# Four pairs of eight by seven products in both feed-forwards of a Conformer block, with other summed tiles

## The chip, the cores and the metric

The kernel runs on one core of one Trainium2 chip. The metric is the device time of one execution in microseconds, from the first to the last instruction with what lies around it. A core has a matrix engine (PE, whose loads of the stationary operand are listed apart as PEld), a vector engine (DVE), an activation engine (ACT), GpSimd (POOL), a sync engine (SP) that issues most loads here, and 16 DMA engines. Each engine works through its own instructions in the order in which they were written into its queue, and waits at an instruction until the semaphores it names have arrived.

## The reference

One layer on 256 tokens of 2048 features: a feed-forward, two mixers side by side (a convolution module and a spatial gating unit), cross-attention into 256 memory tokens, a second feed-forward, and a final norm. All arithmetic is float32. The part that matters here:

```python
def swiglu_ffn(h, w_in, w_out):
    gate, up = jnp.split(h @ w_in, 2, axis=-1)
    return (jax.nn.silu(gate) * up) @ w_out

h = rms_norm(x, ffn1_norm[l])
x = x + MACARON_SCALE * swiglu_ffn(h, ffn1_w_in[l], ffn1_w_out[l])
...
h = rms_norm(x, ffn2_norm[l])
x = x + MACARON_SCALE * swiglu_ffn(h, ffn2_w_in[l], ffn2_w_out[l])
```

`w_in` is 2048 x 11264 and `w_out` 5632 x 2048, so the two feed-forwards hold most of the layer's weights.

## The kernel before

**Three matmuls for one product.** Every float32 operand is split into a rounded half and what is left. ACT casts the rounded half, DVE subtracts it from the original to get the rest, and a product is three matmuls: rounded by rounded, rounded by rest, rest by rounded (`three`, L317 to L319; `by_two`, L330 to L333). For a weight tile this is `parts` (L396 the cast, L397 the subtraction); the tile of 128 x 1024 goes into one of a few buffers, `hl`, `ring` and, in the first feed-forward, `more`, that are used in turn: six in the first feed-forward, five in the second. Loads go to `raw` buffers (four, and parts of the tile `spare`), also in turn, issued by SP (L407).

**Groups.** The product `h @ w_in` is done in 11 groups, j = 0 to 10. A group takes 512 columns of gate and 512 of up, and adds over 16 tiles of 128 features (k = 0 to 15), that is, 8 pairs. Group 0 is done tile by tile, 12 matmuls a tile. Groups 1 to 10 follow a pattern over their pairs, `SCSCSCCC` before the change:

- **C** (`eight`): a pair of two tiles by the plain eight products, 24 matmuls. Each tile is split by `parts`, unless it is a *summed* tile.
- **S** (`seven`): the 2 x 2 block product (two token halves by two column halves) by seven products instead of eight, 21 matmuls. DVE forms sums of the weight blocks first: L464 and L465 into `sums`, L471 into the first tile's buffer, L478 into the second's; and `parts` splits `sums`, the first tile, the second tile and half of it again. The sums on the token side are made once (`sides`) during group 0.

**Summed tiles** (`summed`) spare DVE the subtraction: ACT writes the negative of the rounded half into the place of the rest (L425) and the rounded half beside it (L426), and a DMA issued by GpSimd (L427) adds the weights from memory onto the negative. These tiles have buffers of their own, `hl_s` and a second one. In the second feed-forward the second buffer is given up from group 8 on, where its space is taken by the results of groups 9 and 10. `sums_at` lists which tiles are made this way, three in a group, k = 2, 7, 13.

**The end of a group.** Seven banks of PSUM collect the products, named 1 to 7, and 8. After the last S pair, `joins_sevens` reads banks 1, 6, 5, 7 and 5 again (ACT copies bank 1 at L515; DVE adds at L516 to L519). After the last pair DVE adds banks 2, 4, 3 and 8 (L544, four times) and `give` applies the gate (ACT L504, DVE L506, two of each). The next group takes the banks in the order in which they come free.

**The output product** of the first feed-forward (`out_block`, twice) uses the same two kinds of pairs over 22 pairs; its loads turn among four `raw`, four `raws_out`, and, from step 8 of the first block on, two `raw_out` buffers, whose space is that of the last groups' results and comes free when these have been transposed. The tile `sums_out` lies there too.

The order on every engine is made by the scheduler of the framework, from the order of the code; `tc.issue_after` ties an instruction behind another.

Of the kernel before, what the change touches and what calls it, by code (L numbers as in the profile page):

```python
# [11 lines left out]
F32 = mybir.dt.float32  # L12
# [5 lines left out]
P = 128  # L18
# [15 lines left out]
SCALE = float(HD) ** -0.5  # L34


PATTERNS = ("SCSCSCCC", "SCSCSCCC")

SUMMED = ((2, 7, 13), (2, 7, 13))

# [35 lines left out]
def layer(ctx: ExitStack, tc: tile.TileContext, a: dict):  # L78
# [262 lines left out]
    class FeedForward:  # L341
# [60 lines left out]
        def raw(self, j, k):  # L402
            i = self.raw_at % (4 + len(self.raws))
            self.raw_at += 1
            raw = wraw.tile([P, 1024], F32, name="raw") if i < 4 else self.raws[i - 4]

            nc.sync.dma_start(out=raw, in_=self.w_in[j, :, k] if j < NG else self.w_out[j - NG, :, k])  # L407
            return raw

        def buffer(self, at):  # L410
# [7 lines left out]
        def summed(self, at):  # L418

            if at >= len(self.sums_at):  # L420
                return
            j, k = self.sums_at[at]
            raw, hl = self.raws_summed[self.buffer(at)], self.hls[self.buffer(at)]
            nc.sync.dma_start(out=raw, in_=self.w_in[j, :, k])
            nc.scalar.activation(out=hl[:, 1], in_=raw, func=AF.Copy, scale=-1.0)  # L425
            nc.scalar.copy(out=hl[:, 0], in_=raw)  # L426
            nc.gpsimd.dma_start(out=hl[:, 1], in_=self.w_in[j, :, k], accum_op=ALU.add)  # L427

        def sides(self, i):

# [90 lines left out]
        def group(self, j, r, after=()):  # L521
            if self.pair and j == NG - 2:
                both = self.high_pool.tile([P, 2, 2, G], F32, name="h_pair", tag="pair")
                self.h[NG - 2:] = [both[:, i] for i in range(2)]
            b = {}
            self.begun = set()
            self.banks(b, "57612348")
            after = list(after)
            p1, u2, u4, u5 = self.u
            n = len(self.pattern)  # L530
            for p, c in enumerate(self.pattern):
                if c == "S":
                    self.seven(j, p, b, p == self.spairs[-1])
                    if p == self.spairs[-1]:
                        self.joins_sevens(b, p1, u2, u4, u5)
                else:
                    late = p > self.spairs[-1] and len(after) > 0
                    self.eight(j, p, b, p == n - 1, late)
                    if p > self.spairs[-1] + 1:
                        for _ in range(2):  # L540
                            if after:
                                after.pop(0)()
            for acc, u in (("2", p1), ("4", u2), ("3", u4), ("8", u5)):
                nc.vector.tensor_tensor(out=u, in0=u, in1=b[acc], op=ALU.add)  # L544
            self.give(j, (p1, u2), (u4, u5), r)
# [58 lines left out]
        def run(self, before, after, root, more=None, early=False):  # L604
            acc = token_accs()
            sums = self.pattern_sums
            self.sums_at = [(j, k) for j in range(1, NG) for k in sums if j < NG - 1 or k < min(14, sums[-1])]
            for k in range(KD):
                if k == 0 and early:
                    w = self.early(before)  # L610
                else:
                    before(k)
                    w = self.parts(self.raw(0, k))
                begin = [(t, g) for t in range(2) for g in range(2)] if k == 0 else []
                by_two(acc, self.x_hl[:, k], w[:, 0], w[:, 1], k, begin, k == KD - 1)
                after(k)
                if k == 13:
                    r = root()
                    nc.scalar.activation(out=st.tile([P, 1], F32, name="warm"), in_=ones[:, 0:1], func=AF.Silu)
                    self.summed(0)  # L620
            self.give(0, [acc[t][0] for t in range(2)], [acc[t][1] for t in range(2)], r)
            if more is not None:
                more()
            if len(self.hls) > 1:
                self.summed(1)
            turns = [self.turn(i) for i in range(2 * NG)]
            for j in range(1, NG):
                if j < NG - 1:
# [52 lines left out]
    with ExitStack() as stack:  # L681
# [7 lines left out]
        def x_more(k):  # L689
            if k == 6:  # L690
                nc.sync.dma_start(out=pv, in_=a["pv"])
            if k in (2, 4, 6, 8):
                x_squares(k // 2 - 1)
            if k in (6, 9, 12):
                ff.sides(k // 3 - 2)

        def x_root():
            nc.vector.tensor_tensor(out=r_x, in0=tot[:, 0], in1=tot[:, 1], op=ALU.add)
# [48 lines left out]
        def turns_first(i):  # L747
# [8 lines left out]
            if i == 8:  # L756
                stack.enter_context(ff.late)
                ff.high.close()
                pool = rest["pool"] = stack.enter_context(tc.tile_pool(name="ffn1", bufs=1, reuse_waits="tile"))
                ff.sums = pool.tile([P, 1024], F32, name="sums_out")  # L760
                ff.raws += [pool.tile([P, 1024], F32, name=f"raw_out{q}") for q in range(2)]

        def result():
            return rest["pool"].tile([P, 2, 2 * G], F32, name="o", bufs=2)
# [2 lines left out]
            return [turning(o, 2 * i * P, joins(8 * n + 2 * i)) for i in range(4)]  # L767

        o = ff.out_block(0, result, turns_first, next_turn)
        ff.raws = ff.raws[4:]  # L770
        xT = xt.tile([P, KD, T], F32, name="xT", tag="x")
        for k in range(0, KD, 8):
            nc.gpsimd.dma_start(out=xT[:, k:k + 8], in_=a["xT"][:, k:k + 8])
# [412 lines left out]
    with ExitStack() as stack:  # L1186
# [13 lines left out]

        h = ff.of
        def first_beside(k):
            if k in (6, 9, 12):
                ff.sides(k // 3 - 2)

        turns = ff.run(lambda k: None, first_beside, lambda: rms_cols(ss, D, "r_x2"))
        put(0.3, *[turn(0, i, j) for i in range(4) for j in range(8)])
# [153 lines left out]
```

## Time and profile before

| what | us |
|---|---|
| median of 3 runs | 2098.36 |
| lowest and highest of them | 2094.91, 2098.84 |
| the profiled execution | 2097.01 |
| its span, from the first to the last instruction | 2095.2 |

The granted clock of the matrix engine is 0.999 of full speed over the span. In a row of a timeline the first number is the start in us from the span's start, the second the duration, then the engine, the source line and the operation with its output and inputs. In rows of waits the three numbers are the sum in us, the count and the longest. In rows of windows each engine's busy time is followed by the count of its instructions.

The first feed-forward's groups 1 to 9 lie at about 51 to 424 us, its output product at about 466 to 730 us, the second feed-forward's groups 1 to 9 at about 1425 to 1799 us.

### The profile page before, as it was taken

What the parts mean: (1) busy time and instruction counts of PE and PEld (TensorE: products, weight loads), DVE (VectorE), ACT (ScalarE), POOL (GpSimd) and SP (SyncE); (2) the same over time, 40 slices, a digit from 0 to 9 for tenths busy, and PEclk for the clock granted to TensorE, in tenths of its full rate; (3) what the DMA queues carried; (4) which work ended last, traced back from release to release, by engine and by line L of the source; (5) the groups of instructions that cost most, each with busy time, mean ns of one, the idle gap of its engine ahead of it and who ended that gap; (6) DMA issues with size and microseconds to landing.
All of it is one profiled execution on the core that took longest, in us unless ns stands there. A gap on an engine that the chain in (4) does not pass through costs nothing.

```text
span 2095.2 us, 26732 instructions
## 1 busy us (share of the span) xinstructions
PE 2080.0 (99%) x9765; PEld 1738.5 (83%) x9765; DVE 1621.0 (77%) x2300; ACT 1175.0 (56%) x1472; POOL 67.7 (3%) x83
## 2 busy tenths in 40 slices
PE   9999999999999999999999999999999999999998
PEld 8888888888788888888888898888888888888886
DVE  7888887877777679989877666778888878787754
ACT  8665666555546554445664455556665656554443
POOL 0000000000000000000000000000000000000000
PEclk9999999999999999999999999999999999999999
DMA  9787778755457566555555544677777777556664
GB/s 366 242 260 249 227 226 263 229 182 202 169 201 233 181 237 203 183 180 185 181 195 191 186 157 130 215 269 221 233 242 245 225 221 235 176 163 203 195 193 152
DMA packets 122532, 442.35 MB, mean 211 GB/s; under 512 B 13600, under 2 KB 13984, under 8 KB 122016
## 3 DMA queue, kind: packets, MB, share of 16 engines
q1 hardware_dynamic: 113184, 407.08, 56.4%
q0 software_dynamic: 8640, 32.51, 8.3%
q8 instruction: 76, 1.25, 0.2%
q10 hardware_dynamic: 576, 1.06, 0.1%
q14 instruction: 56, 0.46, 0.1%
HBM read 438.49 MB, written 2.10 MB: 210 GB/s over the span
## 4 chain that ended last, share of the span: by engine, by line
PE 81%; issue 15%; DMA 2%; POOL 1%; ACT 1%; DVE 1%; SPq 0%; DVEq 0%; POOLq 0%; ACTq 0%
PE acc L331 9%; PE acc L333 9%; PE acc L330 9%; PE acc L204 8%; PE acc L203 8%; PE acc L202 8%; PE acc L153 8%; PE acc L161 4%; PE acc L318 2%; PE acc L319 2%; PE acc L317 2%; PE aux L305 1%; POOL hl_s L427 1%; PE acc L1278 1%; PE acc L1277 1%
## 5 line engine op out<-in xcount | busy, mean ns | idle before, releaser
L123 ACT CAST hl<-raw 128x1024 fp32r<-128x1024 f32 (+1 forms) x315 | 327.1, 1040 | 356.1 <-PE acc L204 194.7
L124 DVE TENSOR_TENSOR hl<-raw,hl 128x1024 fp32r<-128x1024 f32 (+1 forms) x315 | 381.2, 1212 | 166.8 <-ACT hl L123 165.4
L397 DVE TENSOR_TENSOR hl<-raw,hl 128x1024 fp32r<-128x1024 f32 (+1 forms) x144 | 164.6, 1145 | 51.2 <-ACT hl L396 49.9
L396 ACT CAST hl<-raw 128x1024 fp32r<-128x1024 f32 (+1 forms) x144 | 141.0, 988 | 110.2 <-PE acc L333 51.4
L397 DVE TENSOR_TENSOR hl<-spare,hl 128x1024 fp32r<-128x1024 f32 (+1 forms) x128 | 146.9, 1152 | 37.3 <-ACT hl L396 34.6
L396 ACT CAST hl<-spare 128x1024 fp32r<-128x1024 f32 (+1 forms) x128 | 126.2, 993 | 73.3 <-PE acc L333 25.4
L331 PE MATMUL acc<-hl,x_hl 128*128 128x512 f32 x408 | 148.2, 391 | 0.1
L330 PE MATMUL acc<-hl,x_hl 128*128 128x512 f32 x408 | 142.4, 391 | 0.0
L333 PE MATMUL acc<-hl,x_hl 128*128 128x512 f32 x408 | 126.6, 389 | 0.0
L396 ACT CAST ring<-spare 128x1024 fp32r<-128x1024 f32 (+1 forms) x81 | 80.5, 998 | 59.3 <-issue 20.4
L397 DVE TENSOR_TENSOR ring<-spare,ring 128x1024 fp32r<-128x1024 f32 (+1 forms) x81 | 93.3, 1157 | 14.8 <-ACT ring L396 13.6
L203 PE MATMUL acc<-hl,x_hl 128*128 128x512 f32 x256 | 100.6, 393 | 0.0
L203 PE MATMUL acc<-hl,m_hl 128*128 128x512 f32 x256 | 100.3, 392 | 0.0
L204 PE MATMUL acc<-hl,m_hl 128*128 128x512 f32 x256 | 100.2, 392 | 0.0
L204 PE MATMUL acc<-hl,x_hl 128*128 128x512 f32 x256 | 99.9, 390 | 0.0
L331 PE MATMUL acc<-ring,x_hl 128*128 128x512 f32 x248 | 91.4, 389 | 0.0
L202 PE MATMUL acc<-hl,m_hl 128*128 128x512 f32 x256 | 90.9, 392 | 0.0
L202 PE MATMUL acc<-hl,x_hl 128*128 128x512 f32 x256 | 90.2, 392 | 0.0
L330 PEld LDWEIGHTS acc<-hl,x_hl 128*128 128x128 f32 x408 | 76.6, 188 | 16.2 <-ACT hl L396 0.4
L333 PEld LDWEIGHTS acc<-hl,x_hl 128*128 128x128 f32 x408 | 76.7, 188 | 16.0
L331 PEld LDWEIGHTS acc<-hl,x_hl 128*128 128x128 f32 x408 | 76.3, 188 | 16.4 <-DVE hl L397 0.8
L330 PE MATMUL acc<-ring,x_hl 128*128 128x512 f32 x248 | 88.8, 389 | 0.0
(515 smaller groups left out, 5115.2 us busy)
## 6 DMA issues: line engine op xcount, KB each, us to landing
spare<-in_ffn_w_in SPq DMA_DIRECT2D x185, 512.0 KB, 6.8
raw<-in_ffn_w_in SPq DMA_DIRECT2D x156, 512.0 KB, 6.3
raw<-in_ffn_w_out SPq DMA_DIRECT2D x135, 512.0 KB, 4.0
hl_s<-in_ffn_w_in POOLq DMA_DIRECT2D x44, 512.0 KB, 8.7
raw<-in_w_mix_vg SPq DMA_DIRECT2D x32, 512.0 KB, 4.5
raw<-in_w_k SPq DMA_DIRECT2D x32, 512.0 KB, 3.6
raw<-in_w_v SPq DMA_DIRECT2D x32, 512.0 KB, 4.3
raw<-in_w_mix_out SPq DMA_DIRECT2D x32, 512.0 KB, 4.6
```

What stands on the lines that cost most here:

```text
L123: nc.scalar.copy(out=hl[:, 0, :size], in_=raw[:, :size])
L124: newest[0] = nc.vector.tensor_tensor(out=hl[:, 1, :size], in0=raw[:, :size], in1=hl[:, 0, :size].bitcast(F32), op=ALU.subtract)
L153: done = nc.tensor.matmul(acc, lhsT=hi[:, k], rhs=xs[k], start=first and k == 0, stop=last and k == kk - 1, skip_group_check=True,)
L161: done = nc.tensor.matmul(acc[:, 0], lhsT=lo[:, k], rhs=xs[k][:, 0], start=False, stop=last and k == kk - 1, skip_group_check=True,)
L202: nc.tensor.matmul(acc[t], lhsT=x[:, 0, s], rhs=hi[:, k], start=k0 + k == 0, stop=False)
L203: nc.tensor.matmul(acc[t], lhsT=x[:, 0, s], rhs=lo[:, k], start=False, stop=False)
L204: nc.tensor.matmul(acc[t], lhsT=x[:, 1, s], rhs=hi[:, k], start=False, stop=k0 + k == nk - 1)
L330: nc.tensor.matmul(acc[t][g], lhsT=x[:, 0, s], rhs=hi[:, cols[g]], start=(t, g) in first, stop=False)
L331: nc.tensor.matmul(acc[t][g], lhsT=x[:, 0, s], rhs=lo[:, cols[g]], start=False, stop=False)
L333: nc.tensor.matmul(acc[t][g], lhsT=x[:, 1, s], rhs=hi[:, cols[g]], start=False, stop=last)
L396: self.cast = nc.scalar.copy(out=hl[:, 0, :n], in_=raw[:, :n])
L397: newest[0] = nc.vector.tensor_tensor(out=hl[:, 1, :n], in0=raw[:, :n], in1=hl[:, 0, :n].bitcast(F32), op=ALU.subtract)
```

## The change

The pattern of groups 1 to 9 becomes `SCSCSCSC` in both feed-forwards: the seventh pair goes from C to S. Group 10 keeps `SCSCSCCC` (`LAST`). The summed tiles are k = 2, 6, 10, 14 in the first feed-forward (2, 6, 10 in its group 10). In the second they are 2, 7, 11 in groups 1 to 7, and 2, 10 in groups 8 to 10. The token-side sums are made for four pairs, after tiles 4, 7, 10 and 13 of group 0. The first two summed tiles are tied behind the last load and the last cast that stand ahead of them in the code (`summed_then`). The two `raw_out` buffers join the turn after the first output block instead of at its step 8, and replace the four `raws_out` there.

```diff
-PATTERNS = ("SCSCSCCC", "SCSCSCCC")
-
-SUMMED = ((2, 7, 13), (2, 7, 13))
+PATTERNS = ("SCSCSCSC", "SCSCSCSC")
+
+LAST = "SCSCSCCC"
+
+SUMMED = ((2, 6, 10, 14), (2, 7, 11))
+ALONE = (2, 10)
+
+SIDES = (4, 7, 10, 13)
...
-            nc.sync.dma_start(out=raw, in_=self.w_in[j, :, k] if j < NG else self.w_out[j - NG, :, k])
+            self.load = nc.sync.dma_start(out=raw, in_=self.w_in[j, :, k] if j < NG else self.w_out[j - NG, :, k])
...
+        def summed_then(self, at):
+
+            with tc.issue_after(self.load.ins), tc.issue_after(self.cast.ins):
+                self.summed(at)
...
-            n = len(self.pattern)
-            for p, c in enumerate(self.pattern):
+            pattern = self.pattern if j < NG - 1 else LAST
+            n, done = len(pattern), pattern.rindex("S")
+            for p, c in enumerate(pattern):
                 if c == "S":
-                    self.seven(j, p, b, p == self.spairs[-1])
-                    if p == self.spairs[-1]:
+                    self.seven(j, p, b, p == done)
+                    if p == done:
                         self.joins_sevens(b, p1, u2, u4, u5)
...
+            if self.pair:
+
+                self.sums_at = [at for at in self.sums_at if at[0] < 8] + [(j, k) for j in range(8, NG) for k in ALONE]
...
-                    self.summed(0)
+                    self.summed_then(0)
...
-                self.summed(1)
+                self.summed_then(1)
...
-            if k in (6, 9, 12):
-                ff.sides(k // 3 - 2)
+            if k in SIDES:
+                ff.sides(SIDES.index(k))
...
-                ff.raws += [pool.tile([P, 1024], F32, name=f"raw_out{q}") for q in range(2)]
+                rest["raws"] = [pool.tile([P, 1024], F32, name=f"raw_out{q}") for q in range(2)]
...
-        ff.raws = ff.raws[4:]
+        ff.raws = rest["raws"]
```

DVE at the end of group 1 of the second feed-forward, before the change (a row is a source line, an operation, and its output and inputs; `acc` and `aux` are banks of PSUM, `hl` and `ring` weight buffers, `h_...` the group's result):

```order
L518 TENSOR_TENSOR spare<-spare,aux 128x512
L397 TENSOR_TENSOR hl<-spare,hl 128x1024
L519 TENSOR_TENSOR spare<-spare,acc 128x512
L464 TENSOR_TENSOR spare<-raw 128x512
L465 TENSOR_TENSOR spare<-raw 128x512
L397 TENSOR_TENSOR hl<-spare,hl 128x1024
L471 TENSOR_TENSOR raw<-spare,raw 128x512
L397 TENSOR_TENSOR hl<-spare,hl 128x1024
L478 TENSOR_TENSOR spare<-spare 128x512
L397 TENSOR_TENSOR ring<-spare,ring 128x512
L544 TENSOR_TENSOR spare<-spare,acc 128x512 x4
L506 SCALAR_TENSOR_TENSOR h_11165<-spare,r_x_11436,h_11165 128x512
```

The same place in the changed kernel, whose lines stand some ten further down (L526 to L529 are the joins, L555 the last adds, L402 the split, L474, L475, L481 and L488 the sums, L516 the gate):

```order
L528 TENSOR_TENSOR spare<-spare,aux 128x512
L402 TENSOR_TENSOR ring<-spare,ring 128x1024
L481 TENSOR_TENSOR raw<-spare,raw 128x512
L555 TENSOR_TENSOR spare<-spare,acc 128x512 x2
L529 TENSOR_TENSOR spare<-spare,acc 128x512
L488 TENSOR_TENSOR spare<-spare 128x512
L516 SCALAR_TENSOR_TENSOR h_11233<-spare,r_x_11512,h_11233 128x512
L555 TENSOR_TENSOR spare<-spare,acc 128x512 x2
L402 TENSOR_TENSOR ring<-raw,ring 128x1024
L402 TENSOR_TENSOR hl<-spare,hl 128x512
L402 TENSOR_TENSOR hl<-spare,hl 128x1024 x2
```

The last join, which stood eight rows ahead of the last adds with a whole pair's sums and splits between, now stands between the second and the third of them, and of the next group's first pair of seven the last sum and its split come behind.

SP in the output blocks of the first feed-forward, before the change:

```order
L407 DMA raw<-in_ffn_w_out 128x1024 x3
L407 DMA raws_out<-in_ffn_w_out 128x1024 x4
L407 DMA raw<-in_ffn_w_out 128x1024 x4
L407 DMA raws_out<-in_ffn_w_out 128x1024 x4
L407 DMA raw_out_3961<-in_ffn_w_out 128x1024
L407 DMA raw_out_3962<-in_ffn_w_out 128x1024
L407 DMA raw_out_3961<-in_ffn_w_out 128x1024
L407 DMA raw<-in_ffn_w_out 128x1024 x2
```

And in the changed kernel:

```order
L412 DMA raws_out<-in_ffn_w_out 128x1024 x4
L412 DMA raw<-in_ffn_w_out 128x1024 x4
L412 DMA raws_out<-in_ffn_w_out 128x1024 x4
L412 DMA raw<-in_ffn_w_out 128x1024 x4
L412 DMA raws_out<-in_ffn_w_out 128x1024 x3
L412 DMA raw_out_4024<-in_ffn_w_out 128x1024
L412 DMA raw_out_4025<-in_ffn_w_out 128x1024
L412 DMA raws_out<-in_ffn_w_out 128x1024 x2
```

The first load into a `raw_out` buffer stood behind 29 loads of the output product's weights and stands behind 30; before, it was for a tile of the first block, now for one of the second.

More of the change, by code (lines that the diff above doesn't have):

```diff
@@ L529, in group @@
             p1, u2, u4, u5 = self.u
-            n = len(self.pattern)
-            for p, c in enumerate(self.pattern):
+            pattern = self.pattern if j < NG - 1 else LAST
+            n, done = len(pattern), pattern.rindex("S")
+            for p, c in enumerate(pattern):
                 if c == "S":
-                    self.seven(j, p, b, p == self.spairs[-1])
-                    if p == self.spairs[-1]:
+                    self.seven(j, p, b, p == done)
+                    if p == done:
                         self.joins_sevens(b, p1, u2, u4, u5)
                 else:
-                    late = p > self.spairs[-1] and len(after) > 0
+                    late = p > done and len(after) > 0
                     self.eight(j, p, b, p == n - 1, late)
-                    if p > self.spairs[-1] + 1:
+                    if p > done + 1:
                         for _ in range(2):
@@ L1202, in first_beside @@
         def first_beside(k):
-            if k in (6, 9, 12):
-                ff.sides(k // 3 - 2)
+            if k in SIDES:
+                ff.sides(SIDES.index(k))
         turns = ff.run(lambda k: None, first_beside, lambda: rms_cols(ss, D, "r_x2"))
```

## The prediction

> **What bounds the kernel now.** I read the page first, for the engine that is never idle, then the busy time by stretches over the groups that the change touches, then single starts on TensorE and VectorE there, and last who waits for whom.
>
> ```profile
> span 2095.2 us, 26732 instructions
> PE 2080.0 (99%) x9765; PEld 1738.5 (83%) x9765; DVE 1621.0 (77%) x2300; ACT 1175.0 (56%) x1472; POOL 67.7 (3%) x83
> PE 81%; issue 15%; DMA 2%; POOL 1%; ACT 1%; DVE 1%; SPq 0%; DVEq 0%; POOLq 0%; ACTq 0%
> ```
>
> PE is busy for 2080.0 of 2095.2 us, and the chain that ends last runs along it. A busy PE may hide slow matmuls, so the groups come next: nine of the first feed-forward, nine of the second.
>
> ```profile
> core 0: us, PE busy (x) PEld busy (x) DVE busy (x) ACT busy (x) POOL busy (x), PEclk, DMA share, GB/s
> 51.00:424.50 373.50, 373.50 (x1649) 309.27 (x1649) 309.63 (x371) 232.89 (x257) 24.38 (x28) 1.00 0.77 240
> 1425.00:1799.00 374.00, 372.18 (x1640) 307.26 (x1638) 307.92 (x368) 231.72 (x250) 22.66 (x26) 1.00 0.76 236
> ```
>
> PE has no gap in the first and 1.8 us in the second, at full clock. VectorE is the runner-up: 309.63 / 9 = 34.4 us of a group of 41.5, 307.92 / 9 = 34.2 in the second, so it idles 7.1 and 7.3 us a group. ACT (25.8 us a group) and the DMA share (0.77) have more room. The same product of three groups in a row gives PE's price of a matmul:
>
> ```profile
> 133.55 0.39 PE L317 MATMUL acc<-hl,ring 128*128 128x512 f32 x1
> ...
> 175.03 0.39 PE L317 MATMUL acc<-hl,ring 128*128 128x512 f32 x1
> ...
> 216.51 0.39 PE L317 MATMUL acc<-hl,ring 128*128 128x512 f32 x1
> ```
>
> A group is 3 pairs of 21 matmuls and 5 of 24, 183 in all; two groups take 82.96 us, so a matmul costs 0.2267 us start to start (the 0.39 is its pipelined length) and a group 41.48 us.
>
> **Term 1, matmuls.** A pair by seven products has three matmuls fewer than one by eight. 18 groups x 3 = 54 of them go: 54 x 0.2267 = **-12.2 us**, all on the engine that sets the end. A group is then 180 x 0.2267 = 40.8 us. The Trainium skill (TensorE: Matmul & The Clock Gate, part 1) gives a warm matmul of 512 columns N / 2.4 GHz + 2.5 ns = 0.2157 us; by that the term would be 11.6 us. The trace has 0.2267, and decides.
>
> **Term 2, what VectorE gets for it.** Its own price per instruction, start to start in a stretch without waits:
>
> ```profile
> 1500.29 2.47 DVE L544 TENSOR_TENSOR spare<-spare,acc 128x512 f32<-128x512 f32 x4
> 1502.67 0.75 DVE L506 SCALAR_TENSOR_TENSOR h<-spare,r_x,h 128x512 f32<-128x512 f32 x1
> 1503.34 1.22 DVE L397 TENSOR_TENSOR ring<-spare,ring 128x1024 fp32r<-128x1024 f32 x1
> ...
> 1506.27 1.22 DVE L397 TENSOR_TENSOR hl<-spare,hl 128x1024 fp32r<-128x1024 f32 x1
> 1507.40 0.69 DVE L464 TENSOR_TENSOR spare<-raw 128x512 f32<-128x512 f32 x1
> 1508.01 0.69 DVE L465 TENSOR_TENSOR spare<-raw 128x512 f32<-128x512 f32 x1
> 1508.61 1.22 DVE L397 TENSOR_TENSOR hl<-spare,hl 128x1024 fp32r<-128x1024 f32 x1
> ```
>
> 1024 columns cost 1.13 us, 512 cost 0.605, an add out of PSUM 2.38 / 4 = 0.6, L506 0.67. A pair by seven products needs five of 512 and three of 1024: 6.43 us. A tile of the other kind needs one of 1024 (1.13), and none if it is a summed tile. First feed-forward: one such pair more, and 4 tiles left to split instead of 7: +6.43 - 3 x 1.13 = +3.0, so 34.4 + 3.0 = 37.4 of 40.8 us. Second, groups 1 to 7: 5 tiles instead of 7, +4.2, 38.4 of 40.8. Its groups 8 and 9 have two summed tiles instead of three: +5.3, 39.5 of 40.8. VectorE stays under PE everywhere, but its idle time must shrink from 7.1 to 3.4, and from 7.3 to 2.4 and 1.3 us. Whether it can depends on what that idle time is. In the second feed-forward:
>
> ```profile
> DVE hl L397 <- ACT hl L396: 25.7, 21, 3.1
> DVE ring L397 <- ACT ring L396: 15.7, 14, 3.1
> DVE spare L464 <- DMA spare<-in_ffn_w_in: 9.9, 5, 2.9
> DVE spare L464 <- DMA raw<-in_ffn_w_in: 7.5, 4, 2.0
> ```
>
> 41.4 us are waits for the rounded half from ACT, the rest mostly for loads. And ACT in turn waited there for:
>
> ```profile
> ACT hl L396 <- PE acc L333: 23.5, 18, 1.7
> ACT ring L396 <- PE acc L333: 14.5, 12, 1.7
> ...
> ACT hl L396 <- DVE raw L478: 7.1, 5, 2.1
> ACT ring L396 <- DVE spare L478: 6.7, 4, 2.1
> ACT hl L396 <- DVE spare L478: 4.9, 3, 2.4
> ...
> ACT ring L396 <- DVE raw L478: 2.9, 3, 2.1
> ```
>
> Most of it is PE not having freed a weight buffer: VectorE is ahead, and that wait goes once it is not. What stays is the hand-back inside a seven-product pair (VectorE's L478, ACT's cast, VectorE's split): 21.6 us, 2.4 a group, for four pairs instead of three 3.2. **Bounds:** below, all of it is filled by other work, 0. Above, all 3.2 stay: 38.4 + 3.2 is 0.8 over 40.8 in seven groups, 39.5 + 3.2 is 1.9 over in two, 9.4 us; the first feed-forward (37.4 + 3.2 = 40.6) still fits. Since the new order puts joins and other pairs' sums between the hand-backs, I take about the middle: **+5 us** of PE stalls.
>
> The joins (L516 to L519) cost no more instructions, but only 24 matmuls (5.4 us) instead of 72 (16.3) now lie between the last pair of seven and the next group. In the order they are 4 x 0.6 = 2.4 us beside three or four splits, about 6 us, and the next group starts on the banks that come free first; cover is the last tile's second half and those products. I cost them at nothing beyond the 5 us. ACT gets 44 instructions of a microsecond or less more, by estimate 2 us a group on 25.8, under PE. The fourth set of sides lies in group 0, under 192 matmuls (43.5 us): nothing.
>
> **Term 3, summed tiles.** The only PE waits in those groups:
>
> ```profile
> PE acc L331 <- DMA hl_s<-in_ffn_w_in: 1.9, 3, 0.8
> ```
>
> They lie in groups 8 and 9 of the second feed-forward, where one buffer serves tiles 2, 7 and 13. From the end of tile 2 to tile 7 PE has two tiles and a pair of seven, 2 x 2.72 + 4.76 = 10.2 us, and was 0.5 to 0.8 short: the refill takes about 11 us. After the change the same buffer is used 8 tiles apart everywhere (2 and 10 there; two buffers in turn in the first feed-forward): three tiles and two pairs, 17.7 us. The waits go: **-1.9 us**; bounds -1.9 and 0. The tie of the first two tiles behind a load and a cast adds a place in ACT's and SP's queues, some 20 us before their use by PE (six tiles and the first pair): nothing.
>
> **Term 4, output block.** A stretch of 25 us (PE busy, clock, DMA share, GB/s), SP's load in it, and PE's wait:
>
> ```profile
> 525.00:550.00 25.00, 23.49 (x105) 1.00 0.29 94
> 519.99 15.11 SPq L407 DMA_DIRECT2D raw_out<-in_ffn_w_out  x3
> 533.53 1.20 PE L330 MATMUL acc<-more_out,hB 128*128 128x512 f32 x4 [0.45 <-ACT more_out L396]
> ```
>
> SP, in order, sat for 15 us at loads into raw_out, whose space the last transposes still held; the DMA share fell to 0.29 and PE lost 1.5 us. These two buffers now come into turn only in the second output block. In SP's order 30 loads still stand ahead of them, but with eight buffers in turn the last of these go out only when PE has used some 22 tiles (11 pairs of 5.44 us), and by then the transposes are done. **-1.4 us**; bounds -1.5 and, if SP meets the same wait, 0.
>
> **Sum:** 2097.0 - 12.2 + 5 - 1.9 - 1.4 = **2086.5 us**, from the profiled execution (2097.01, 1.35 below the median of the runs shown, 2098.36).
>
> **Rivals.** (a) *VectorE is already the bound at full durations.* The group view gives them:
>
> ```profile
> L397 DVE TENSOR_TENSOR hl<-raw,hl 128x1024 fp32r<-128x1024 f32 x123 | 150.1, 1223 | 33.3 <-ACT hl L396 31.9
> L464 DVE TENSOR_TENSOR spare<-raw 128x512 f32<-128x512 f32 x34 | 23.5, 691 | 21.9 <-DMA raw<-in_ffn_w_in 21.9
> L544 DVE TENSOR_TENSOR spare<-spare,acc 128x512 f32<-128x512 f32 x80 | 50.4, 683 | 14.1 <-PE acc L333 14.1
> ```
>
> A group of the second feed-forward would be 17 x 1.223 + 20 x 0.691 + 8 x 0.683 + 2 x 0.75 = 41.6 us, 42.8 in groups 8 and 9: nothing gained there, 3 us lost. The first would fit (40.3): -6.1. With term 4, 2097.0 - 6.1 + 3 - 1.4 = 2092.5. Against it: the starts above are 1.13 apart, not 1.22. [...]
>
> (b) *The hand-backs do not fill.* If VectorE keeps its whole 41.4 us of waits for ACT, 4.6 a group, a group of the second feed-forward takes 38.4 + 4.6 = 43.0 instead of 41.5, and 44.1 in two: +15.7. The first, with 3.4 us of room, keeps its -6.1, and term 4 its -1.4: **2105, slower**. It decides for slower from an idle time of 3.9 us a group, where the second loses what the rest gains. Against it: most of these waits are PE's own pace.
>
> (c) *The stalls eat the gain*: between (a) and (b), idle near 3 to 4 us, 2094 to 2101.
>
> (d) *Summed tiles come late in the first feed-forward*, with 4 a group. Refill rows:
>
> ```profile
> hl_s<-in_ffn_w_in POOLq DMA_DIRECT2D x44, 512.0 KB, 8.7
> ```
>
> It needs 8 us longer than before to miss 17.7; at 1 us for each of 36 tiles, 2097.0 - 15.5 + 36 = 2117 at worst. The DMA share rises only by a twentieth (20 tile loads for 19).
>
> **How the numbers follow.** Forecast 0.65; (a) 0.12; (c) 0.13; (b) 0.07; (d) 0.03. The range goes from all stalls gone (2081.5) to the upper bound of term 2 with terms 3 and 4 at nothing (2094.2) and a little of the runs' scatter: 2081 to 2095, leaving out (b), (d) and most of (c). A measurement tells about 0.2%, 4.2 us, from no change: faster 0.79, same 0.13, slower 0.08.
>
> **What would show it.** Groups of the first feed-forward at 40.8 us on PE without a gap; VectorE busy for 92 to 96% of both; in the second, PE gaps of half a microsecond a group put down to VectorE's split; no wait for a summed tile; a full PE between 520 and 540 us. PE gaps over 0.7 us a group in the second feed-forward, or any in the first, would make term 2 wrong.

## The result, and the profile after

The changed kernel takes 2106.61 us (median of 6 runs, 2103.99 to 2107.09), the kernel before 2096.62 us (6 runs). The ratio is 1.0045, with a 95% interval of 1.0033 to 1.0057: about 10 us slower, where 10 us faster had been forecast. The profiled execution took 2103.99 us against 2097.01. It is the fastest of the six, so the stages below account for 7 of the 10 us.

The page of the changed kernel, span, busy time and the chain that ended last:

```profile
span 2102.2 us, 26762 instructions
PE 2075.7 (99%) x9711; PEld 1724.7 (82%) x9711; DVE 1680.6 (80%) x2410; ACT 1202.3 (57%) x1522; POOL 74.7 (4%) x91
PE 74%; issue 17%; DMA 4%; DVE 3%; POOL 1%; ACT 1%; SPq 0%; DVEq 0%; POOLq 0%; ACTq 0%
```

The 54 matmuls are gone (9765 to 9711). But VectorE, which was 1% of that chain, is 3% of it now, and PE has 74% in place of 81%. The two stretches of nine groups, and the one of the output block:

```profile
51.00:424.50 373.50, 370.51 (x1625) 304.09 (x1624) 332.53 (x417) 250.89 (x284) 32.23 (x37) 1.00 0.85 253
1425.00:1799.00 374.00, 362.89 (x1569) 291.86 (x1569) 329.42 (x406) 228.04 (x255) 20.01 (x23) 1.00 0.73 225
525.00:550.00 25.00, 23.70 (x107) 18.38 (x106) 20.08 (x27) 13.25 (x17) 0.00 (x0) 1.00 0.40 145
```

PE had no gap in the first stretch and has 3.0 us; in the second it had 1.8 us and has 11.1. The second holds fewer matmuls than before in the same time (1569 for 1640): those groups became longer, not shorter. The gaps are not all that PE lost: by estimate 1569 matmuls at 0.2267 us are 355.7 us, and PE is busy for 362.89. Some 7 us more are hidden there, since a matmul is listed with 0.39 us and a late start of the next one by up to 0.16 us shows no gap. The gate's activations mark the ends of a feed-forward's groups, the `h<-acc` row the end of group 0, the last start of the other rows the end of group 10. Before (count, shortest, median and longest in ns, first and last start):

```profile
L504 ACT ACTIVATE h<-spare,r_x x20: 712/722/728, 91.4 to 469.2; 128x512 f32<-128x512 f32 x20
L504 ACT ACTIVATE h<-acc,r_x x2: 680/684/688, 51.0 to 51.6; 128x512 f32<-128x512 f32 x2
...
L504 ACT ACTIVATE h_pair<-spare,r_x x4: 717/726/727, 1793.1 to 1839.5; 128x512 f32<-128x512 f32 x4
...
L504 ACT ACTIVATE h<-acc,r_x x2: 680/684/687, 1418.3 to 1418.9; 128x512 f32<-128x512 f32 x2
```

After:

```profile
L514 ACT ACTIVATE h<-spare,r_x x20: 714/722/728, 93.6 to 467.1; 128x512 f32<-128x512 f32 x20
L514 ACT ACTIVATE h<-acc,r_x x2: 689/691/693, 50.0 to 51.1; 128x512 f32<-128x512 f32 x2
...
L514 ACT ACTIVATE h_pair<-spare,r_x x4: 715/724/731, 1800.1 to 1846.8; 128x512 f32<-128x512 f32 x4
...
L514 ACT ACTIVATE h<-acc,r_x x2: 682/687/692, 1414.1 to 1414.7; 128x512 f32<-128x512 f32 x2
```

First feed-forward: 469.2 - 51.0 = 418.2 us before, 417.1 after. Second: 421.2 before, 432.7 after. With what lies ahead (-1.0), between them (-2.1, where a wait of PE at 1300 to 1325 us is gone, which nobody had forecast) and behind (-0.3), this is the +7.0 us of the two spans. Each feed-forward has 27 matmuls fewer, 6.1 us at 0.2267. So PE lost 6.1 - 1.1 = 5.0 us more than before in the first and 6.1 + 11.5 = 17.6 us more in the second. (The expectations below read the same ends a little differently: 415.7, 432.9 and 419.4.) What PE waited for in the second feed-forward:

```profile
PE acc L336 <- DMA hl_s<-in_ffn_w_in: 2.7, 2, 1.6
PE aux L322 <- DVE spare L528: 1.6, 2, 0.9
PE acc L336 <- DVE ring L402: 1.5, 3, 0.6
PE acc L322 <- ACT hl L401: 1.5, 2, 1.2
PE acc L322 <- ACT ring L401: 1.4, 2, 1.2
PE acc L335 <- ACT ring L401: 1.2, 2, 0.9
PE acc L322 <- DVE spare L555: 1.0, 2, 0.8
...
```

No one cause stands out: casts, splits, joins (L528), final adds (L555) and a summed tile, each for one to three microseconds. So the first row is not the cause by being first.

### The profile page after: what moved, and what is told of

The parts are those of the page before. It is cut to its first block, busy times and chain, and to the rows that moved or that the text cites. A ratio compares the mean times of both kernels' runs of the same rounds, so it can differ in the third digit from the quotient of the medians.

```text
span 2102.2 us, 26762 instructions
## 1 busy us (share of the span) xinstructions
PE 2075.7 (99%) x9711; PEld 1724.7 (82%) x9711; DVE 1680.6 (80%) x2410; ACT 1202.3 (57%) x1522; POOL 74.7 (4%) x91
## 4 chain that ended last, share of the span: by engine, by line
PE 74%; issue 17%; DMA 4%; DVE 3%; POOL 1%; ACT 1%; SPq 0%; DVEq 0%; POOLq 0%; ACTq 0%
PE acc L208 8%; PE acc L209 8%; PE acc L207 8%; PE acc L158 8%; PE acc L336 7%; PE acc L338 7%; PE acc L335 7%; PE acc L166 4%; DMA raw<-in_ffn_w_in 3%; PE acc L322 2%; PE acc L323 2%; PE acc L324 2%; PE aux L310 1%; DMA spare<-in_ffn_w_in 1%; PE acc L1292 1%
## 5 line engine op out<-in xcount | busy, mean ns | idle before, releaser
L128 ACT CAST hl<-raw 128x1024 fp32r<-128x1024 f32 (+1 forms) x315 | 327.3, 1041 | 356.6 <-PE acc L209 198.9
L129 DVE TENSOR_TENSOR hl<-raw,hl 128x1024 fp32r<-128x1024 f32 (+1 forms) x315 | 381.3, 1212 | 163.7 <-ACT hl L128 162.1
L402 DVE TENSOR_TENSOR hl<-raw,hl 128x1024 fp32r<-128x1024 f32 (+1 forms) x155 | 175.4, 1136 | 52.2 <-ACT hl L401 51.2
L401 ACT CAST hl<-raw 128x1024 fp32r<-128x1024 f32 (+1 forms) x155 | 149.8, 980 | 97.1 <-PE acc L338 44.8
L402 DVE TENSOR_TENSOR hl<-spare,hl 128x1024 fp32r<-128x1024 f32 (+1 forms) x139 | 157.6, 1141 | 24.0 <-ACT hl L401 23.7
L401 ACT CAST hl<-spare 128x1024 fp32r<-128x1024 f32 (+1 forms) x139 | 135.0, 984 | 71.9 <-DVE spare L488 26.4
L336 PE MATMUL acc<-hl,x_hl 128*128 128x512 f32 x336 | 116.5, 391 | 0.2
L335 PE MATMUL acc<-hl,x_hl 128*128 128x512 f32 x336 | 112.5, 391 | 0.1
L402 DVE TENSOR_TENSOR ring<-spare,ring 128x1024 fp32r<-128x1024 f32 (+1 forms) x89 | 101.9, 1150 | 11.1 <-ACT ring L401 10.9
L338 PE MATMUL acc<-hl,x_hl 128*128 128x512 f32 x336 | 105.8, 389 | 0.0
L208 PE MATMUL acc<-hl,x_hl 128*128 128x512 f32 x256 | 100.6, 393 | 0.0
L209 PE MATMUL acc<-hl,x_hl 128*128 128x512 f32 x256 | 99.9, 390 | 0.0
L207 PE MATMUL acc<-hl,x_hl 128*128 128x512 f32 x256 | 90.5, 392 | 0.0
L401 ACT CAST ring<-raw 128x1024 fp32r<-128x1024 f32 (+1 forms) x70 | 66.3, 952 | 38.3 <-PE acc L324 14.2
L432 POOL DMA_DIRECT2D hl_s<-in_ffn_w_in x47 | 41.0, 873 | 1230.4 <-ACT hl_s L430 640.6
L402 DVE TENSOR_TENSOR ring<-raw,ring 128x1024 fp32r<-128x1024 f32 (+1 forms) x70 | 76.7, 1099 | 8.0 <-ACT ring L401 7.8
L336 PE MATMUL acc<-hl_s,x_hl 128*128 128x512 f32 x188 | 73.3, 391 | 3.3 <-DMA hl_s<-in_ffn_w_in 3.3
L336 PEld LDWEIGHTS acc<-hl,x_hl 128*128 128x128 f32 x336 | 62.9, 188 | 14.2 <-DVE hl L402 1.0
```

What stands on the lines that cost most here:

```text
L128: nc.scalar.copy(out=hl[:, 0, :size], in_=raw[:, :size])
L129: newest[0] = nc.vector.tensor_tensor(out=hl[:, 1, :size], in0=raw[:, :size], in1=hl[:, 0, :size].bitcast(F32), op=ALU.subtract)
L207: nc.tensor.matmul(acc[t], lhsT=x[:, 0, s], rhs=hi[:, k], start=k0 + k == 0, stop=False)
L208: nc.tensor.matmul(acc[t], lhsT=x[:, 0, s], rhs=lo[:, k], start=False, stop=False)
L209: nc.tensor.matmul(acc[t], lhsT=x[:, 1, s], rhs=hi[:, k], start=False, stop=k0 + k == nk - 1)
L335: nc.tensor.matmul(acc[t][g], lhsT=x[:, 0, s], rhs=hi[:, cols[g]], start=(t, g) in first, stop=False)
```

## The experiments

All times are medians; the ratio is to the kernel before, run beside each. FF1 and FF2 are the two stage lengths, each from one profiled execution.

| run | us | ratio (95%) | FF1 | FF2 |
|---|---|---|---|---|
| changed kernel | 2106.6 | 1.0045 (1.0033 to 1.0057) | 417.1 | 432.7 |
| pe_order | 2155.4 | 1.0288 (1.0272 to 1.0303) | 442.5 | 462.6 |
| ff1_only | 2094.4 | 0.9992 (0.9983 to 1.0002) | 416.8 | 419.6 |
| joins_free | 2101.9 | 1.0034 (1.0020 to 1.0049) | 417.8 | 429.4 |
| no_handback | 2094.4 | 0.9994 (0.9984 to 1.0003) | 416.2 | 421.8 |
| one_trip | 2084.4 | 0.9944 (0.9929 to 0.9958) | 415.8 | 415.9 |
| dve_more | 2100.7 | 1.0018 (1.0008 to 1.0028) | 420.8 | 427.4 |
| ff2_sum4 | 2105.2 | 1.0043 (1.0028 to 1.0058) | 420.6 | 433.4 |
| ff1_five | 2105.4 | 1.0042 (1.0027 to 1.0057) | 419.9 | 432.5 |
| one_trip_p | 2087.0 | 0.9955 (0.9940 to 0.9970) | 411.7 | 421.0 |
| before_one_trip | 2098.0 | 1.0012 (1.0003 to 1.0022) | 418.6 | 421.1 |
| before_more_trips | 2093.8 | 0.9994 (0.9984 to 1.0003) | 418.2 | 418.4 |
| dve_tiny | 2093.3 | 0.9989 (0.9980 to 0.9998) | 419.3 | 420.3 |
| order_tiny | 2091.2 | 0.9981 (0.9971 to 0.9991) | 418.4 | 419.9 |
| order_same | 2106.5 | 1.0049 (1.0034 to 1.0065) | 420.6 | 430.7 |
| dve_tiny_late | 2089.5 | 0.9971 (0.9960 to 0.9982) | 419.6 | 416.4 |
| one_trip_mix | 2082.1 | 0.9935 (0.9919 to 0.9951) | 411.7 | 416.0 |
| before_tiny | 2097.4 | 1.0007 (0.9997 to 1.0017) | 418.2 | 421.9 |
| mix_tiny | 2082.2 | 0.9930 (0.9915 to 0.9945) | 411.7 | 416.1 |

### First round: where, and which wait

**ff1_only.** `PATTERNS = ("SCSCSCSC", "SCSCSCCC")`, and the summed tiles and sides of before in the second feed-forward.

> The new pattern and four summed tiles in the first feed-forward only; the second has the pattern, the summed tiles and the three sets of sides of before. Every theory that puts the loss into the second feed-forward: its stage back from 432.9 to about 419.4 us, the first stays at 415.7 (before 418.4), total 2092 to 2094. If part of the loss came from elsewhere (ties, output block), it would stay above 2096.

The second feed-forward is back at 419.6 us and the total at 2094.4: the loss lies there. The first gains nothing that can be told from no change. Ten executions share its code and order (the changed kernel, this one, joins_free, no_handback, dve_more, ff2_sum4, dve_tiny, order_tiny, order_same, dve_tiny_late); they give 416.2 to 420.8 us, 418.7 on average, against 418.2 before. The 6.1 us of matmuls went into stalls. One order so gives stage lengths that differ by 4.6 us between single executions: smaller differences in the table's last two columns say nothing by themselves.

**pe_order.** Every matmul of groups 1 to 9 pinned behind the one written before it:

```diff
+    def pin(done):
+        if pinned[0]:
+            tc.keep_in_program_order(done)
...
-        nc.tensor.matmul(acc, lhsT=x[0], rhs=hi, start=first, stop=False)
+        pin(nc.tensor.matmul(acc, lhsT=x[0], rhs=hi, start=first, stop=False))
```

> Groups 1 to 9 of both feed-forwards with TensorE's matmuls pinned to the order in which the code writes them (tile by tile); nothing else changes. In the changed kernel the matmuls of three or four weight tiles alternate. Theory 'order' (weight buffers are handed back late because several tiles are half done at once): the second feed-forward, 432.9 us from its first gate activation to its last in the changed kernel, falls by 8 us or more, total 2090 to 2098. Theory 'VectorE' (its work plus its waits for ACT and loads is longer than a group, whatever the order): the same 2105 or some us more, since a matmul on a low part can no longer be stepped over.

A miss: 49 us slower than the changed kernel. With the written order the next group's products stand at the final adds (L561 here):

```profile
PE acc L328 <- DVE spare L561: 30.5, 13, 3.3
```

The granted clock fell as well, to 0.985 over the span from 0.999; by estimate that is up to 0.014 x 2158.5 = 30 of the 49 us (see the last section). The compiled order, which mixes the matmuls of several tiles, was steering around such waits. It was not bad because it was mixed.

**joins_free**, an edit of one line:

```diff
-                        self.joins_sevens(b, p1, u2, u4, u5)
+                        self.joins_sevens({n: u4 for n in "1567"} if self.pair else b, p1, u2, u4, u5)
```

> Second feed-forward: the copy and four adds behind the last pair of seven read a buffer in SBUF in place of the PSUM banks, so they cost VectorE the same and wait for no matmul, and the banks are free at the last matmul; the sums of the products 1, 5, 6, 7 are left out of its output. Theory 'joins': the 5.8 us of VectorE's waits for the copy and TensorE's 2.6 us for joins and final adds go, and with them half of the loss or more: 2092 to 2098. Theory 'VectorE' or 'order': under 4 us of gain, 2102 to 2105.

It gained 4.7 us, which lies between the two expectations.

**no_handback.** Two sums written to places that no cast reads:

```diff
-            nc.vector.tensor_tensor(out=one[:, lo], in0=sums[:, lo], in1=two[:, hi], op=ALU.add)
+            apart = self.pair and j < NG
+            nc.vector.tensor_tensor(out=sums[:, lo] if apart else one[:, lo], in0=sums[:, lo], in1=two[:, hi], op=ALU.add)
...
-            nc.vector.tensor_tensor(out=two[:, lo], in0=two[:, lo], in1=one[:, lo], op=ALU.subtract)
+            nc.vector.tensor_tensor(out=one[:, lo] if apart else two[:, lo], in0=two[:, lo], in1=one[:, lo], op=ALU.subtract)
```

> Second feed-forward: the two sums that a pair of seven makes in place are written to buffers that no cast reads (same count and size on VectorE), so two of its three hand-backs VectorE - ACT - VectorE go; products 6 and 4 get other weights. Theory 'hand-backs' (the prediction's rival b): VectorE's waits for ACT in that stage fall from 30.7 to 15 us or less and the total to 2090 to 2097. Theory 'order', or 'loads late': less than 4 us, 2101 to 2105.

The time was 2094.4, 12 us back, as the prediction's rival (b) had it. At this point the hand-backs looked like the cause. But the sign that was to come with it did not: VectorE's waits for ACT's casts in that stage, which should have fallen from 30.7 us to 15 or less, were 29.7 us for `hl` and 10.4 for `ring`, 40.1 in all. The time fell while the waits that were to explain it grew.

### Second round: hand-backs, work or buffers

**dve_more.** VectorE gets 2.4 us a group of work that leads nowhere.

```diff
+            if self.pair:
+                nc.vector.tensor_tensor(out=sums[:, hi], in0=sums[:, hi], in1=two[:, hi], op=ALU.add)
```

> Second feed-forward: one add of 512 columns more per pair of seven (its result is read by nothing), 4 x 0.605 = 2.4 us of VectorE per group, in no chain of casts. Theory 'VectorE is the bound': all of it shows, 9 to 10 groups x 2.4 = 20 us or more, 2125 or later. Theory 'hand-backs' (the loss is latency between two in-order engines, VectorE still has idle time of its own): under half of it, 2107 to 2116.

More work made the kernel 5.9 us **faster** than the changed kernel. In the second feed-forward VectorE is busy for 377.18 us of this stretch, in the changed kernel for 353.28 (the stretch, then the busy time of PE, PEld and DVE; first dve_more, then the changed kernel):

```profile
1425.00:1825.00 400.00, 394.19 (x1700) 315.95 (x1699) 377.18 (x475) 246.46 (x277) 21.73 (x25) 1.00 0.73 224
1425.00:1825.00 400.00, 387.83 (x1678) 312.18 (x1678) 353.28 (x433) 244.12 (x273) 20.87 (x24) 1.00 0.73 223
```

So the amount of VectorE's work is not the bound, and rival (a) falls: at 94% busy VectorE feeds PE better. No theory so far had expected this sign.

**ff2_sum4** (`SUMMED = ((2, 6, 10, 14), (2, 6, 10, 14))`) and **ff1_five** (the line `ff.ring.append(more[:, :2])` left out):

> Second feed-forward: four summed tiles (2, 6, 10, 14) instead of three in groups 1 to 7, as in the first; per group one split of 1.13 us on VectorE less, one cast more on ACT. Theory 'VectorE is the bound': 7 x 1.1 = 8 us come back, 2097 to 2100. Theory 'hand-backs': the pairs of seven stay as they are, under 4 us, 2102 to 2106.

> First feed-forward with five buffers for cast and split weights, as the second has, in place of six. Theory 'buffers' (the second loses more because it has five): its stage grows from 418 us by 6 us or more, total 2112 or later. Theory 'hand-backs' or 'VectorE': under 3 us, 2106 to 2109.

The times are 2105.2 and 2105.4: one split less in seven groups brings back 1.4 us, and one buffer less in the first feed-forward costs nothing. Six buffers in the second were not tried.

**one_trip.** The same instructions, written so that a pair of seven hands over once. `straight` holds the cast and split of the second raw tile with products 2 and 3, `fourth` the last sum; both stood further down.

```diff
+            early = j < NG
...
+            if early:
+                straight()
+                nc.vector.tensor_tensor(out=one[:, lo], in0=sums[:, lo], in1=two[:, hi], op=ALU.add)
+                fourth()
             w = self.parts(sums)
...
-            nc.vector.tensor_tensor(out=one[:, lo], in0=sums[:, lo], in1=two[:, hi], op=ALU.add)
+            if not early:
+                nc.vector.tensor_tensor(out=one[:, lo], in0=sums[:, lo], in1=two[:, hi], op=ALU.add)
             w = self.parts(one)
...
+            if not early:
+                straight()
+                fourth()
             w = self.parts(two, G)
```

> The changed kernel with the work of a pair of seven in the two input products written in another order, nothing left out: the raw tile (products 2 and 3) is cast and split first, then the two in-place sums follow in one go on VectorE, and then the three remaining casts and splits (5 and 7, 6 and 1, 4); so one round trip VectorE - ACT - VectorE per pair in place of three. Theory 'hand-backs': most of the 12 us that came back when two of the three were taken away (2106.6 to 2094.4) come back here too, in both feed-forwards: 2090 to 2097. If the time was lost for another reason, 2102 to 2108; products 2 and 3 now come first and need banks that the last group frees late, which would show as TensorE's waits for the final adds (over 3 us).

The time is 2084.4, better than expected and faster than both kernels.

### Third round: the converse

**before_more_trips** writes the second sum into the raw tile (`out=two[:, hi]` for `out=sums[:, hi]`, except once at the start); **before_one_trip** is the edit of one_trip on the kernel before.

> The kernel before, second feed-forward: one of the two sums ahead of a pair is written into the raw tile itself, so that products 2 and 3 wait for it too: four round trips per pair in place of three, no instruction more (products 2, 3 and 7 get other weights). Theory 'hand-backs': 29 round trips more, about as many as the change brings there (30), cost 6 us or more: 2103 or later. If it is VectorE's or ACT's work that costs: no change, 2095 to 2099.

> The kernel before with one round trip per pair of seven (the edit of one_trip) and nothing of the change. If the three round trips cost before what they cost after, this kernel gains as much, 10 us or more (2075 to 2087). Theory 'hand-backs beyond the slack': with three pairs VectorE had 7 us of idle time a group and TensorE stands still for less than 7 us in both feed-forwards together, so at most 5 us: 2091 to 2097. The distance to one_trip is then the price of the matmuls taken out, 12.2 us by the prediction's first term.

29 more round trips cost nothing (2093.8), and taking two of three away gained nothing (2098.0). In the kernel before, round trips show no price.

**one_trip_p**: `early = j < NG and p > 0`.

> As one_trip, but the first pair of each group keeps the order sums - tile - sums, so that its products 2 and 3 don't come while the last group still holds their banks. Theory 'hand-backs': three of four pairs are mended, 2084 to 2090; faster than one_trip only if the banks cost something there.

The time is 2087.0; its first feed-forward is the shortest yet, 411.7 us, its second takes 421.0.

**dve_tiny**: the add of dve_more with 16 columns (`G:G + 16` for `hi`).

> As dve_more, with 16 columns in place of 512, so next to no work, in the same places. It asks why dve_more was faster than the changed kernel (2100.7 against 2106.6). If the compile-time order alone did it, this one moves by some microseconds too, to either side, 2098 to 2108; if a wait of an ACT cast for that add did it, 2100 to 2102.

The time is 2093.3, below every number expected: adds of 16 columns, 36 of them in groups 1 to 9, take 13 us off, as much as no_handback. Their work is next to nothing. In the compiled program they change the place of 981 of the 1620 matmuls of the second feed-forward's groups 1 to 9, of 274 of VectorE's 425 instructions and of 125 of ACT's 266. That is also true of no_handback, joins_free and dve_more: each had changed the order, and none can be read as the price of what it takes away or adds.

### Fourth round: the order alone

**order_tiny** and **order_same**: the changed kernel, with `ORDER` a table of the order of PE, VectorE, ACT and SP in the second feed-forward's groups 1 to 9, from dve_tiny (its adds dropped) or from the changed kernel itself.

```diff
+    def ordered(traced):
+
+        for engine, places in ORDER.items():
+            mine = [i for i in traced if str(i.engine) == "EngineType." + engine]
+            row = [mine[int(n)] for n in places.split(",")]
+            for ahead, behind in zip(row, row[1:]):
+                tc.add_manual_dep(
...
+                if j == NG - 1 and self.pair:
+                    ordered(nc.cur_bb.bb.instructions[traced:])
```

> The changed kernel, not an instruction more or less: groups 1 to 9 of its second feed-forward on TensorE, VectorE, ACT and SP are put into the order that they have in dve_tiny (without its adds). Theory 'order': the loss goes as in dve_tiny, 2091 to 2097. Theory 'hand-backs' (or that the small adds themselves helped): all three hand-backs are there as before, 2104 to 2108.

> The control: the same pinning by the same code, with the order of the changed kernel itself. Both theories: 2104 to 2108.

The same instructions take 2091.2 us in one order and 2106.5 in the other. By the traces, order_same runs these four engines in the changed kernel's order from end to end, so the pinning itself costs nothing; order_tiny departs from it only between 1430 and 1840 us. What PE waited for in the second feed-forward, with order_same:

```profile
PE acc L342 <- DMA hl_s<-in_ffn_w_in: 1.8, 2, 1.4
PE acc L328 <- ACT hl L419: 1.4, 2, 1.2
PE acc L328 <- ACT ring L419: 1.4, 2, 1.2
PE acc L341 <- ACT ring L419: 1.4, 3, 0.9
PE acc L342 <- DVE ring L420: 1.1, 3, 0.5
PE aux L328 <- DVE spare L546: 1.0, 2, 0.7
PE acc L328 <- DVE spare L573: 1.0, 2, 0.8
...
```

and with order_tiny:

```profile
PE aux L328 <- ACT ring L419: 1.1, 1, 1.1
PE acc L341 <- ACT ring L419: 1.0, 3, 0.3
PE acc L328 <- ACT ring L419: 0.7, 1, 0.7
PE acc L329 <- DVE ring L420: 0.2, 1, 0.2
PE acc L341 <- ACT hl L419: 0.2, 1, 0.2
```

The waits for a summed tile, the joins and the final adds are gone together, with none of them repaired. The two gate activations at the ends of the stage stand at 1417.3 and 1848.0 us in order_same, and here at

```profile
L532 ACT ACTIVATE h_pair<-spare,r_x x4: 714/721/727, 1787.5 to 1834.6; 128x512 f32<-128x512 f32 x4
...
L532 ACT ACTIVATE h<-acc,r_x x2: 681/686/692, 1414.7 to 1415.3; 128x512 f32<-128x512 f32 x2
```

That is 430.7 us against 419.9: 10.8 of the 13.4 us between the two profiled executions (2105.23 and 2091.83) lie in the stage that was pinned. Another 2.2 lie in the first feed-forward, whose order is the same, within its scatter.

**dve_tiny_late**: the 16 columns behind the pair's last split.

> The 16 dead columns of dve_tiny at the other end of the pair, behind its last split. Theory 'order': some other order, so some other time, anywhere from 2088 to 2108. If it is again 2092 to 2095, the adds as such help.

The time is 2089.5, another order and another time. It does not tell apart whether such adds help as such; order_tiny does, since it has none.

**one_trip_mix**: `early = j < NG and (p > 0 or self.pair)`.

> One round trip per pair in all pairs of the second feed-forward, and in all but a group's first in the first (where one_trip_p had its best stage, 413.0 us, and one_trip its best in the second, 417.3). If stages add up: 2080 to 2083; if the difference of the stages was scatter of one execution: 2083 to 2086.

The time is 2082.1, the fastest version, 14 us below the kernel before beside it (2096.2). Its stages are those of its two parents, 411.7 and 416.0. In the second PE waits for next to nothing (the stretch, then PE's waits in this stage):

```profile
1425.00:1825.00 400.00, 399.17 (x1761) 328.17 (x1760) 361.63 (x450) 254.66 (x283) 20.86 (x24) 1.00 0.74 227
```

```profile
PE acc L322 <- ACT hl L401: 0.4, 2, 0.2
```

**before_tiny** and **mix_tiny**: the adds of dve_tiny in the kernel before and in one_trip_mix.

> The kernel before with the 16 dead columns per pair of seven in the second feed-forward, the edit of dve_tiny. In the compiled order it moves no place on ACT and 235 on TensorE (in the changed kernel 125 and 1002). Theory 'order only where VectorE has little room': within 3 us of before, 2093 to 2099. If any order of this kernel may cost 10 us: outside of that.

> one_trip_mix with the same dead adds in its second feed-forward; they move 10 places on ACT and 349 on TensorE. If the single round trip makes the order matter less, it stays within 3 us of one_trip_mix, 2080 to 2085. If one_trip_mix was a lucky order, 2087 or later.

The times are 2097.4 and 2082.2: both stay where they were. What moved the changed kernel by 13 us moves neither of these by more than 1.3 us. It also moves fewer places in their orders (235 and 349 on PE), so this shows that their orders change little, not that any order of theirs would do.

## Why the prediction was wrong

**Term 1, matmuls, -12.2: right.** 54 fewer ran, and where the stalls are gone their time shows: in one_trip_mix the first feed-forward is 418.2 - 411.7 = 6.5 us shorter than before (6.1 by the term), the second 421.2 - 416.0 = 5.2.

**Term 2, VectorE, +5: the step that failed.** The term set VectorE's work (37.4 to 39.5 us) and its hand-backs (up to 3.2) against a group of 40.8 us, and took what sticks out, at most 9.4 us, as PE's stalls. Measured, they were about 5.0 + 17.6 = 22.6 us, and 5.0 of them in the first feed-forward, which "still fits". The prediction's own sign that term 2 is wrong came too: gaps of PE of 11.1 / 9 = 1.2 us a group in the second feed-forward, where 0.7 was the limit, and 3.0 us in the first, where none was allowed. The sum was of the wrong kind. VectorE was busy for 332.53 / 373.5 = 89% and 329.42 / 374 = 88% of the two stretches, under the 92 to 96% that the prediction wanted to see; it had idle time left while PE stalled, and with 2.4 us of work more in each group (dve_more) PE stalled less. What decided in the second feed-forward was something that the prediction had read, in the order of both kernels, and not priced: the changed program's order was compiled anew, and the queues work it off as it stands. With the same instructions it is worth 2106.5 - 2091.2 = 15.3 us there. The prediction's middle between 0 and 9.4 assumed an order that fills the waits as well as that of before. For the 5.0 us of the first feed-forward the cause stays open: no run gave its instructions another order and nothing else.

The Trainium skill (PSUM — Partial Sum Buffer, Engine vs sequencer instructions) states that the queues of ScalarE, VectorE and GpSimd are strict FIFO. The two orders of one set of instructions agree with it: had each engine taken whatever was ready, the order would hardly have been worth 15.3 us.

**The joins, "nothing beyond the 5 us": not so.** PE waited 1.6 us for them and 1.0 us for the final adds in the second feed-forward; but in order_tiny, with the same joins and the same 24 matmuls behind them, both waits are gone. The shorter cover alone does not make them.

**Term 3, summed tiles, -1.9: not there.** The wait is 2.7 us, once 1.6. The term placed a tile's 12 matmuls in a row and so 17.7 us between two tiles of one buffer. In the compiled order a tile's matmuls lie among others: those of the tile ahead of the longest wait run from 1759.74 to 1768.84 us, and the next tile's begin at 1777.96, only 9 us later. So the buffer comes free late and is wanted soon. In order_tiny and one_trip_mix no such wait is left.

**Term 4, output block, -1.4: not there.** PE had 23.49 us of work in the 25 us from 525 us and has 23.70. SP still stands for as long, and not for the transposes' space but for a split of the tile in its next buffer:

```profile
SPq L412 <- DVE more_out L402: 17.8, 2, 15.9
```

Between 505 and 550 us of the kernel before, SP's longest waits were of that kind already, which the term had not looked up:

```profile
SPq L407 <- DVE more_out L397: 25.3, 5, 10.5
```

The 15.11 us that the term read as a wait for the transposes is a row of three loads into `raw_out`: two went out at 519.99 and 520.46 us, and the wait lay ahead of the third, at 534.77, 10.5 us of it for VectorE's split. This is the bound "SP meets the same wait" that the term named and did not take.

**The rivals.** (a) is out by dve_more. (b) gave 2105, and 2106.6 was measured, but for a reason that does not hold: the changed kernel keeps all its hand-backs in order_tiny and is 5 us faster than the kernel before. That its number came so close is luck. (c), stalls that eat the gain, is the nearest in kind, and too small. (d) did not come: in the first feed-forward PE waited for a summed tile once, 0.7 us.

**Two slips of the working, on which nothing hangs.** A pair by seven is 5 x 0.605 + 3 x 1.13 = 6.415 us, not 6.43, and rival (b) turns slower at an idle time of about 3.7 us a group by its own terms, not 3.9.

**What stays open.** Which places of the order cost, and why it came out so, was not found, and the best order tried for the changed kernel as it is written (2091.2) is still 4.7 us above the forecast. Nor is it settled whether a round trip has a price of its own in the changed kernel: all four versions with one trip in at least three of a group's four pairs and nothing left out (2082.1 to 2087.0) are faster than the eight with three trips in both feed-forwards, nothing left out and an order of the scheduler's or a copy of one (2089.5 to 2106.6; pe_order is not among them), but each is also another order. That little room on VectorE is what makes the order matter is argued from before_tiny, before_one_trip and before_more_trips, which stay within 3 us of the kernel before; no run gave a bad order that much room.

## What to carry to other kernels

Where a scheduler lays out in-order queues and a second engine is left little idle time, a sum of work per group bounds the gain and not the loss; keep the range open by what another order may cost, here 15 us. Before reading an experiment as the price of one cause, add a dead instruction of a few columns and, better, copy the one order onto the other program: if that moves the time as much, the experiment has shown nothing about the wait that it removed. And try writing dependent steps so that they hand over once, the plain tile first and the sums in one go: the four versions of the changed kernel written so are the fastest here, though whether by the single trip or by the order that came with it is not shown.

## What the runs showed of the hardware

In pe_order the matrix engine ran at a lower clock after short waits. After this wait of 2.59 us

```profile
1629.19 0.60 PE L328 MATMUL acc<-ring,x_hl 128*128 128x512 f32 x1 [2.59 <-DVE spare L561]
```

the granted clock of the next 7 us was 0.53 (the number ahead of the last two):

```profile
1620.00:1629.00 9.00, 6.60 (x29) 5.07 (x28) 9.00 (x14) 5.13 (x6) 0.00 (x0) 1.00 0.63 183
1629.00:1636.00 7.00, 5.17 (x12) 3.83 (x13) 6.84 (x11) 1.34 (x2) 0.00 (x0) 0.53 0.44 142
```

So, as an estimate, the wait cost up to 7 x 0.47 = 3.3 us of clock on top, as far as PE had work (it was busy for 5.17 of the 7 us). The Trainium skill (TensorE: Matmul & The Clock Gate, HAM oscillation — how this bites in real kernels) sets the limit at idle gaps of about 3.4 us; here 2.59 us, in a stretch of 9 us in which PE was busy for 6.60, was enough. The waits of the changed kernel, up to 1.6 us, left the clock at 1.00.
